# Low parts of weight tiles by ScalarE and an accumulating DMA in place of VectorE's subtraction

## The chip, the cores and the metric

The kernel runs on one core of a Trainium2 chip. The metric is device time in microseconds of one execution, as the median of three runs. The engines are named as the profile names them: PE (TensorE), with PEld for its weight loads, DVE (VectorE), ACT (ScalarE), POOL (GpSimd) and SP (SyncE, which issues most DMAs).

## The reference

A decoder trunk of two layers over 512 tokens and a width of 1024, all in float32. The first layer mixes tokens with a gated delta rule (DeltaNet), the second with sliding-window attention over one shared key/value projection; each layer ends in a gated MLP with a width-3 causal convolution. What matters here are the large products with weights:

```python
proj = hn @ w_in                       # 1024 x 6176, then conv, delta rule, gate
o @ w_out                              # 2048 x 1024
kv = rmsnorm(h, kv_norm_w) @ w_kv      # 1024 x 512
q = hn @ w_q;  o @ w_o                 # 1024 x 1024 each
u = causal_dwconv(hn @ w_up, conv_w, conv_b)          # 1024 x 5632, twice
gate, val = jnp.split(u, 2, axis=-1)
(jax.nn.silu(gate) * val) @ w_down                    # 2816 x 1024, twice
```

## The kernel before

Activations lie transposed: features on the 128 partitions, the 512 tokens along the free dimension. A float32 product is made of three products in the rounded type float32r. Every operand is split into a high part (rounded to float32r) and a low part (what the rounding left), and `mm3` adds high x high, weight high x activation low, and weight low x activation high into one PSUM bank.

Weights are streamed. `load_stage` lets SP load a block of up to 1024 x 256 weights into a buffer named `stage` (two buffers), as up to eight row blocks of 128. `cast` makes from one half of it (128 output columns) the tiles `whi` and `wlo` (three buffers each): ACT rounds to `whi`, DVE subtracts `whi` from the stage and writes `wlo`. `mm3` then runs three matmuls of 128x512 for each row block, 24 for a tile of eight. The down-projection has tiles of six and of five row blocks, the others of eight. A buffer of `whi` is free again when the last matmul of its tile that reads it (L136) is done, one of `wlo` with the last at L137.

The order of the instructions on each engine is set at build time by a scheduler that works by priorities and an estimate of each instruction's time; each engine then runs its list in order and waits for semaphores. In the DeltaNet stage the table `ORDER` and the shifts `SHIFT` set the priorities of the jobs. POOL has little to do before: it clears tiles, among them parts of `Xg` (L572) in the triangular solve, which it may do only once the matmuls at L555 have read them, and key tiles of attention (L960, L961).

Of the kernel before, what the change touches and what calls it, by code (L numbers as in the profile page):

```python
# [8 lines left out]
F32 = mybir.dt.float32  # L9
F32R = mybir.dt.float32r  # L10
BF16 = mybir.dt.bfloat16
AF = mybir.ActivationFunctionType
ALU = mybir.AluOpType
# [4 lines left out]
P = 128  # L18
# [23 lines left out]
def kernel(  # L42
# [27 lines left out]
    V, S, G, PE, SP = nc.vector, nc.scalar, nc.gpsimd, nc.tensor, nc.sync  # L70
# [6 lines left out]
    def nm(s):  # L77
        cnt[0] += 1
        return f"{s}_{cnt[0]}"
# [33 lines left out]
        return cp.tile(list(shape), dt, name=nm(s))  # L113


    def load_stage(w, r0, kt, c0):
        st = wpool.tile([P, 8, 256], F32, tag="stage", bufs=2, name=nm("stage"))
        SP.dma_start(
            st[:, :kt, :],
            w[r0 : r0 + kt * P, c0 : c0 + 256].rearrange("(k p) c -> p k c", p=P),  # L120
        )
        return st

    def cast(st, kt, half, m=P):
        hi = wpool.tile([P, 8, P], F32R, tag="whi", bufs=3, name=nm("whi"))
        lo = wpool.tile([P, 8, P], F32R, tag="wlo", bufs=3, name=nm("wlo"))
        src = st[:, :kt, half * P : half * P + m]
        S.copy(hi[:, :kt, :m], src)  # L128
        V.tensor_tensor(lo[:, :kt, :m], src, hi[:, :kt, :m].bitcast(F32), op=ALU.subtract)  # L129
        return hi, lo  # L130

# [101 lines left out]
    st = [{} for _ in range(4)]  # L233
    def project(c0, i):
        if c0 not in held_stage:
            held_stage[c0] = load_stage(win, 0, 8, c0)
        ps = bank("d")
        mm3(ps[:], cast(held_stage[c0], 8, i), KD, xh, xl)
        return ps
# [13 lines left out]
    S.dma_start(gst[:, :, 0:16], win[:, c_b : c_b + 16].rearrange("(k p) c -> p k c", p=P))  # L253
    S.dma_start(gst[:, :, 32:48], win[:, c_b + 16 : c_b + 32].rearrange("(k p) c -> p k c", p=P))
    gw = cast(gst, KD, 0, m=48)
    gps = bank("d")
    mm3(gps[:48, :], gw, KD, xh, xl, m=48)
# [518 lines left out]
    for m2 in range(KD // 2):  # L776
        sts = [load_stage(a_w_out[0], 1024 * u, 8, 256 * m2) for u in range(2)]
        for j in range(2):
            m = 2 * m2 + j
            ps = bank("d")  # L780
            for u in range(2):
                w = cast(sts[u], 8, j)
                mm3(ps[:], w, 8, yh[8 * u : 8 * u + 8], yl[8 * u : 8 * u + 8], first=u == 0, last=u == 1)
            V.tensor_tensor(hT[m], hT[m], ps[:], op=ALU.add)
# [44 lines left out]
    def ffn(l, h, last=False):  # L829
# [22 lines left out]
        for t0, t1 in ((0, 12), (12, 22)):  # L852
            gh, gl = [], []
            for t in range(t0, t1, 2):
                if l == 0 and t == 6:
                    bias_rows()
                sg = load_stage(wup, 0, 8, t * P)
                sv = load_stage(wup, 0, 8, DFF + t * P)
                gp, lp = wide("G"), wide("L")
                for j in range(2):  # L860
                    a = up(cast(sg, 8, j), t + j, "ga")
                    S.activation(a[:], a[:], AF.Silu)  # L862
                    b = up(cast(sv, 8, j), NF + t + j, "va")
                    V.tensor_tensor(b[:], a[:], b[:], op=ALU.mult)
                    split(b[:], gp[:, j, :], lp[:, j, :])
                    gh.append(gp[:, j, :])
                    gl.append(lp[:, j, :])
            ku = (t1 - t0) // 2
            for m2 in range(KD // 2):
                sts = [load_stage(wdn, (t0 + u * ku) * P, ku, 256 * m2) for u in range(2)]  # L870
                for j in range(2):
                    m = 2 * m2 + j
                    ws = [cast(sts[u], ku, j) for u in range(2)]
                    if last and t1 == NF and m == KD - 1:
                        final(h, lambda ps, ts, u: down(ps, ws, ku, gh, gl, ts, u))
                        continue
                    ps = bank("d")
                    for u in range(2):
                        down(ps[:], ws, ku, gh, gl, slice(0, T), u)
                    V.tensor_tensor(h[m], h[m], ps[:], op=ALU.add)  # L880
# [247 lines left out]
```

## Time and profile before

| | |
|---|---|
| median of 3 runs | 1462.74 us (1460.52 to 1462.97) |
| the profiled execution | 1458.21 us, of which the span 1456.4 us |
| PE busy | 1432.3 us (98%) |
| DVE busy | 953.5 us (65%) |
| ACT busy | 718.9 us (49%) |
| POOL busy | 20.1 us (1%) |
| DMA, mean over the span | 105 GB/s |
| HBM read / written | 134.65 MB / 16.80 MB |
| granted TensorE clock, mean | 0.996 |

Busy times of different engines overlap, so they don't add up to the span. A line of a group gives source line, engine, operation, output<-inputs, shape and count, then the busy time and the mean of one, then how long the engine stood idle just before these instructions and who ended that. A line of waits gives the engine and what it wanted to do, whom it waited for, the total, the number of waits and the longest. The DMA share is the mean busy share of the core's 16 DMA engines; packets whose times overlap can bring it over 100%.

### The profile page before, as it was taken

What the parts mean: (1) busy time and instruction counts of PE and PEld (TensorE: products, weight loads), DVE (VectorE), ACT (ScalarE), POOL (GpSimd) and SP (SyncE); (2) the same over time, 40 slices, a digit from 0 to 9 for tenths busy, and PEclk for the clock granted to TensorE, in tenths of its full rate; (3) what the DMA queues carried; (4) which work ended last, traced back from release to release, by engine and by line L of the source; (5) the groups of instructions that cost most, each with busy time, mean ns of one, the idle gap of its engine ahead of it and who ended that gap; (6) DMA issues with size and microseconds to landing.
All of it is one profiled execution on the core that took longest, in us unless ns stands there. A gap on an engine that the chain in (4) does not pass through costs nothing.

```text
span 1456.4 us, 19545 instructions
## 1 busy us (share of the span) xinstructions
PE 1432.3 (98%) x7519; PEld 1163.6 (80%) x7519; DVE 953.5 (65%) x1661; ACT 718.9 (49%) x1406; POOL 20.1 (1%) x47
## 2 busy tenths in 40 slices
PE   7999999999999999999999999999999999999998
PEld 5778877888877788888888888877788888888887
DVE  5896885978844436776247765777757774366754
ACT  7764564656646424443224444578744443234433
POOL 1000000000000000000010000000000000000000
PEclk9999999999999999999999999999999999999999
DMA  5334254163366523232232234221132322322222
GB/s 154 92 99 112 78 171 119 59 189 110 98 189 209 163 87 108 69 114 87 87 116 91 83 95 130 89 79 44 58 105 69 116 83 86 122 87 87 94 73 94
DMA packets 163074, 152.71 MB, mean 105 GB/s; under 512 B 24165, under 2 KB 150694, under 8 KB 162982
## 3 DMA queue, kind: packets, MB, share of 16 engines
q1 hardware_dynamic: 160722, 151.27, 33.3%
q8 instruction: 59, 0.97, 0.3%
q10 hardware_dynamic: 2259, 0.20, 0.2%
q14 instruction: 34, 0.27, 0.1%
HBM read 134.65 MB, written 16.80 MB: 104 GB/s over the span
## 4 chain that ended last, share of the span: by engine, by line
PE 95%; DMA 3%; ACT 1%; DVE 1%; issue 0%; ACTq 0%; DVEq 0%; SPq 0%
PE d L135 27%; PE d L137 27%; PE d L136 26%; PE s L585 2%; PE p L1043 1%; PE s L600 1%; PE g L1038 1%; PE s L625 1%; PE p L608 1%; PE s L562 1%; PE p L555 1%; PE s L1013 1%; PE g L450 1%; PE g L671 1%; PE g L375 1%; DMA ol<-od 0%
## 5 line engine op out<-in xcount | busy, mean ns | idle before, releaser
L135 PE MATMUL d<-xh,whi 128*128 128x512 f32 x1192 | 475.8, 400 | 0.1
L137 PE MATMUL d<-xh,wlo 128*128 128x512 f32 x1192 | 473.3, 398 | 0.0
L136 PE MATMUL d<-xl,whi 128*128 128x512 f32 x1192 | 471.6, 396 | 0.0
L128 ACT CAST whi<-stage 128x1024 fp32r<-128x1024 f32 (+2 forms) x236 | 230.5, 979 | 337.6 <-PE d L136 318.6
L129 DVE TENSOR_TENSOR wlo<-stage,whi 128x1024 fp32r<-128x1024 f32 (+2 forms) x236 | 267.3, 1133 | 120.4 <-ACT whi L128 114.3
L137 PEld LDWEIGHTS d<-xh,wlo 128*128 128x128 f32 x1192 | 224.4, 188 | 50.5 <-issue 1.4
L136 PEld LDWEIGHTS d<-xl,whi 128*128 128x128 f32 x1192 | 224.3, 188 | 48.2 <-issue 1.2
L135 PEld LDWEIGHTS d<-xh,whi 128*128 128x128 f32 x1192 | 224.7, 188 | 46.1 <-issue 0.7
L842 DVE TENSOR_TENSOR sz<-d,p6s 128x512 f32<-128x512 f32 x58 | 40.0, 689 | 62.9 <-PE d L137 61.0
L227 DVE SCALAR_TENSOR_TENSOR acc<-d,cwc,acc 128x511 f32<-128x511 f32 (+2 forms) x96 | 70.7, 740 | 9.3 <-ACT acc L224 8.8
L862 ACT ACTIVATE dt<-dt 128x512 f32<-128x512 f32 x44 | 27.8, 632 | 83.5 <-DVE dt L847 83.5
L135 PE MATMUL d<-sy,whi 128*128 128x512 f32 (+1 forms) x148 | 57.6, 390 | 0.0
L137 PE MATMUL d<-sy,wlo 128*128 128x512 f32 (+1 forms) x148 | 57.5, 389 | 0.0
L135 PE MATMUL d<-kT,whi 128*128 128x512 f32 (+1 forms) x146 | 57.5, 396 | 0.0
L136 PE MATMUL d<-sy,whi 128*128 128x512 f32 (+1 forms) x148 | 57.0, 385 | 0.0
L137 PE MATMUL d<-kT,wlo 128*128 128x512 f32 (+1 forms) x146 | 57.0, 390 | 0.0
L136 PE MATMUL d<-qT,whi 128*128 128x512 f32 (+1 forms) x146 | 56.8, 389 | 0.0
L847 DVE SCALAR_TENSOR_TENSOR va<-sz,fcw,va 128x511 f32<-128x511 f32 (+1 forms) x58 | 43.4, 748 | 2.7 <-ACT va L845 1.7
L847 DVE SCALAR_TENSOR_TENSOR dt<-sz,fcw,dt 128x511 f32<-128x511 f32 (+1 forms) x58 | 43.4, 748 | 1.2 <-ACT dt L845 0.2
L842 DVE TENSOR_TENSOR zl<-d,p6s 128x512 f32<-128x512 f32 x30 | 20.7, 689 | 33.4 <-PE d L137 33.1
L507 DVE TENSOR_TENSOR sT<-sT,p6s 64x31 f32<-64x31 f32 (+15 forms) x124 | 40.9, 330 | 2.0
L501 DVE TENSOR_TENSOR p6s<-sN,sT 64x31 f32<-64x31 f32 (+15 forms) x124 | 40.9, 330 | 1.8
(377 smaller groups left out, 2116.8 us busy)
## 6 DMA issues: line engine op xcount, KB each, us to landing
stage<-in_ffn_w_up_dram SPq DMA_DIRECT2D x44, 1024.0 KB, 5.1
stage<-in_a_w_in_dram SPq DMA_DIRECT2D x23, 1024.0 KB, 5.4
stage<-in_ffn_w_down_dram SPq DMA_DIRECT2D x16, 768.0 KB, 4.3
stage<-in_ffn_w_down_dram SPq DMA_DIRECT2D x16, 640.0 KB, 4.1
stage<-in_a_w_out_dram SPq DMA_DIRECT2D x8, 1024.0 KB, 5.0
zd<-sz SPq DMA_DIRECT2D x16, 256.0 KB, 2.1
od<-o SPq DMA_DIRECT2D x16, 256.0 KB, 2.5
stage<-in_b_w_q_dram SPq DMA_DIRECT2D x4, 1024.0 KB, 5.0
```

The source lines that it names most:

```text
L128: S.copy(hi[:, :kt, :m], src)
L129: V.tensor_tensor(lo[:, :kt, :m], src, hi[:, :kt, :m].bitcast(F32), op=ALU.subtract)
L135: PE.matmul(ps, hi[:, k, :m], xh[k], start=first and k == 0, stop=False)
L136: PE.matmul(ps, hi[:, k, :m], xl[k][:], start=False, stop=False)
L137: PE.matmul(ps, lo[:, k, :m], xh[k], start=False, stop=last and k == kt - 1)
L227: V.scalar_tensor_tensor(acc[:, d:], ps[:, : T - d], col, acc[:, d:], op0=ALU.mult, op1=ALU.add)
L501: V.tensor_tensor(tv, N[:, s, s + 1 : 32].unsqueeze(2).to_broadcast([64, n, m]), Tm[:, s : s + 1, 0:m].to_broadcast([64, n, m]), op=ALU.mult,)
L507: V.tensor_tensor(Tm[:, s + 1 : 32, 0:m], Tm[:, s + 1 : 32, 0:m], tv, op=ALU.subtract)
L585: PE.matmul(x[:, si], t[:, i, cs], S0[:, si], start=True, stop=True)
L842: V.tensor_tensor(u[:], ps[:], rs[:], op=ALU.mult)
L847: V.scalar_tensor_tensor(acc[:, d:], u[:, : T - d], tap(2 - d, t), acc[:, d:], op0=ALU.mult, op1=ALU.add)
L862: S.activation(a[:], a[:], AF.Silu)
```

## The change

`load_stage` remembers where in HBM a stage came from. `cast` no longer subtracts on DVE: ACT, after rounding to `whi`, makes a second pass that writes the negative of `whi` into `wlo`, and POOL issues a DMA that reads the same weights from HBM a second time and adds them to `wlo` in place. The first stage, which is loaded in two halves, and the small tile of gate weights keep DVE's subtraction. The weights reach the DMA in runs of 128 float32, 512 bytes, where a stage load has runs of 256.

```diff
+    origin = {}
+
     def load_stage(w, r0, kt, c0):
         st = wpool.tile([P, 8, 256], F32, tag="stage", bufs=2, name=nm("stage"))
-        SP.dma_start(
-            st[:, :kt, :],
-            w[r0 : r0 + kt * P, c0 : c0 + 256].rearrange("(k p) c -> p k c", p=P),
-        )
+        src = w[r0 : r0 + kt * P, c0 : c0 + 256].rearrange("(k p) c -> p k c", p=P)
+        SP.dma_start(st[:, :kt, :], src)
+        origin[id(st)] = (st, src)
         return st
...
         src = st[:, :kt, half * P : half * P + m]
         S.copy(hi[:, :kt, :m], src)
+        if id(st) in origin and m == P:
+            S.activation(lo[:, :kt, :m], hi[:, :kt, :m].bitcast(F32), AF.Copy, scale=-1.0)
+            G.dma_start(lo[:, :kt, :m], origin[id(st)][1][:, :, half * P : half * P + m], accum_op=ALU.add)
+            return hi, lo
         V.tensor_tensor(lo[:, :kt, :m], src, hi[:, :kt, :m].bitcast(F32), op=ALU.subtract)
```

Lines from L128 on move down by one to five: the cast of `whi` is L129 after the change, the negation L131, the DMA L132, and `mm3` L140 to L142.

ACT's list in the first layer's up-projections, before (`va`, `dt` are the convolved value and gate rows, `kT`, `sy` take rounded results):

```order
L128 CAST whi_5884<-stage_5804 128x1024
L845 ACTIVATE va_5797<-sz_5795,normc_101,fcw_371 128x512
L140 CAST kT_5654<-va_5797 128x512
L128 CAST whi_5920<-stage_5806 128x1024
L845 ACTIVATE dt_5841<-zl_5839,normc_101,fcw_371 128x512
L862 ACTIVATE dt_5841<-dt_5841 128x512
```

The same place after:

```order
L129 CAST whi_5964<-stage_5882 128x1024
L850 ACTIVATE va_5875<-sz_5873,normc_101,fcw_371 128x512
L131 ACTIVATE wlo_5965<-whi_5964 128x1024
L145 CAST kT_5728<-va_5875 128x512
L129 CAST whi_6001<-stage_5884 128x1024
L850 ACTIVATE dt_5920<-zl_5918,normc_101,fcw_371 128x512
L131 ACTIVATE wlo_6002<-whi_6001 128x1024
L867 ACTIVATE dt_5920<-dt_5920 128x512
```

The negation stands behind the next activation of the convolution, not directly behind its cast.

POOL's list at the end of the DeltaNet stage, after (before, the two clearings of `Xg` follow each other with nothing between them and the next clearing):

```order
L132 DMA wlo_4450<-in_a_w_in_dram 128x8x128
L132 DMA wlo_4679<-in_a_w_out_dram 128x8x128
L577 MEMSET Xg 32x8x32 x2
L132 DMA wlo_4708<-in_a_w_out_dram 128x8x128
L132 DMA wlo_4739<-in_a_w_out_dram 128x8x128
```

The DMAs of the low parts share POOL's queue with the clearings, which wait for PE.

## The prediction

> **What bounds the kernel now.** I read the page first (shares of the span and the chain that ended last), then the busy time by stage, then the groups of the two conversion lines, then one period of the timeline, and last the DMA queues.
>
> ```profile
> span 1456.4 us, 19545 instructions
> PE 1432.3 (98%) x7519; PEld 1163.6 (80%) x7519; DVE 953.5 (65%) x1661; ACT 718.9 (49%) x1406; POOL 20.1 (1%) x47
> PE 95%; DMA 3%; ACT 1%; DVE 1%; issue 0%; ACTq 0%; DVEq 0%; SPq 0%
> ```
>
> TensorE is busy for 98% of the span and carries 95% of the chain. Only 1456.4 - 1432.3 = 24.1 us are not its own. The stretches below are the DeltaNet stage, a stretch of up-projections, one of down-projections, and the attention heads.
>
> ```profile
> 0.00:450.00 450.00, 436.12 (x2907) 356.91 (x2908) 336.91 (x713) 273.66 (x666) 11.74 (x31) 0.99 0.42 125
> 530.00:660.00 130.00, 130.00 (x570) 105.66 (x569) 85.39 (x109) 54.93 (x69) 0.00 (x0) 1.00 0.30 95
> 660.00:740.00 80.00, 80.00 (x351) 65.65 (x350) 36.61 (x46) 22.81 (x29) 0.00 (x0) 1.00 0.31 100
> 960.00:1050.00 90.00, 90.00 (x577) 66.02 (x574) 67.40 (x219) 70.39 (x219) 0.00 (x0) 1.00 0.16 48
> ```
>
> The columns are busy PE, PEld, DVE, ACT and POOL, the granted clock, the DMA share and GB/s. In the two middle rows PE never idles at clock 1.00; 570 matmuls in 130 us are 228 ns each. The kernel is bound by the rate of its matmuls, so work taken from DVE buys almost nothing by itself. What matters is whether the new way of making a low part still arrives before its matmuls.
>
> **What is taken out and put in.** These groups are the rounding on ACT and the subtraction on DVE, by shape:
>
> ```profile
> L128 ACT CAST whi<-stage 128x1024 fp32r<-128x1024 f32 x172 | 180.4, 1052 | 193.0 <-PE d L136 178.4 <-DMA stage<-in_a_w_in_dram 4.2 <-issue 4.0
> L128 ACT CAST whi<-stage 128x768 fp32r<-128x768 f32 x32 | 26.8, 836 | 84.2 <-PE d L136 84.2
> L128 ACT CAST whi<-stage 128x640 fp32r<-128x640 f32 x32 | 23.3, 729 | 60.4 <-PE d L136 56.0 <-PE d L137 3.0 <-DMA stage<-in_ffn_w_down_dram 1.4
> L129 DVE TENSOR_TENSOR wlo<-stage,whi 128x1024 fp32r<-128x1024 f32 x172 | 210.3, 1224 | 64.0 <-ACT whi L128 58.2 <-PE d L135 1.6 <-PE d L137 0.3
> L129 DVE TENSOR_TENSOR wlo<-stage,whi 128x768 fp32r<-128x768 f32 x32 | 30.7, 958 | 38.1 <-ACT whi L128 38.0
> L129 DVE TENSOR_TENSOR wlo<-stage,whi 128x640 fp32r<-128x640 f32 x32 | 26.3, 822 | 18.2 <-ACT whi L128 18.0
> ```
>
> 234 tiles change: 170 of eight row blocks, 32 of six, 32 of five (the first two tiles and the small gate tile keep the subtraction). DVE loses 170 x 1.224 + 32 x 0.958 + 32 x 0.822 = 265 us. ACT gains a pass of the same shapes; taken at the price of the cast it is 170 x 1.052 + 32 x 0.836 + 32 x 0.729 = 229 us, so ACT goes to 948 us, 65% of the span. Its densest stretch, the attention heads, holds 8 of these tiles: (70.4 + 8 x 1.05)/90 = 88%. As PE is fully busy there, I cost the ACT pass itself at 0; its cover is the two tiles that are ready ahead, and if that were gone it would be the 8.4 us of that stretch. What DVE's relief can return is at most PE's waits for DVE:
>
> ```profile
> PE g L314 <- DVE sz L282: 2.5, 1, 2.5
> PE g L774 <- DVE va L672: 2.5, 1, 2.5
> PE s L585 <- DVE S L611: 0.8, 1, 0.8
> PE d L908 <- DVE xh L922: 0.2, 1, 0.2
> PE s L213 <- DVE xl L145: 0.2, 1, 0.2
> PE g L927 <- DVE ol L923: 0.2, 1, 0.2
> ```
>
> That is 6.4 us in all, between 0 and -6.4; I take 0, since the long ones wait for a chain of which DVE is one link. SP's loads wait less long for a free stage buffer:
>
> ```profile
> SPq L118 <- DVE wlo L129: 852.0, 99, 29.6
> ```
>
> They will now wait for ACT's cast, about 1.2 us earlier. PE waits for no stage, so this is worth 0.
>
> **The new path of a low part.** One period of an up-projection, then two casts each of the six- and five-block down-projections:
>
> ```profile
> 604.05 1.05 ACT L128 CAST whi<-stage 128x1024 fp32r<-128x1024 f32 x1 [1.00 <-PE d L136]
> 605.01 0.82 ACT L845 ACTIVATE va<-sz,normc,fcw 128x512 f32<-128x512 f32 x1
> 609.54 1.05 ACT L128 CAST whi<-stage 128x1024 fp32r<-128x1024 f32 x1 [0.35 <-PE d L136]
> ...
> 605.14 1.23 DVE L129 TENSOR_TENSOR wlo<-stage,whi 128x1024 fp32r<-128x1024 f32 x1 [0.17 <-ACT whi L128]
> ...
> 693.90 0.84 ACT L128 CAST whi<-stage 128x768 fp32r<-128x768 f32 x1 [3.33 <-PE d L136]
> 697.98 0.84 ACT L128 CAST whi<-stage 128x768 fp32r<-128x768 f32 x1 [3.23 <-PE d L136]
> ...
> 898.54 0.73 ACT L128 CAST whi<-stage 128x640 fp32r<-128x640 f32 x1 [2.71 <-PE d L136]
> 901.97 0.73 ACT L128 CAST whi<-stage 128x640 fp32r<-128x640 f32 x1 [1.29 <-PE d L136]
> ```
>
> Each cast starts when PE lets go of its buffer, so PE's time per tile is 609.54 - 604.05 = 5.49 us, 4.08 and 3.43. With three buffers a tile has two such periods until its matmuls: 11.0, 8.2 and 6.9 us. DVE finished the low part at 606.37, 2.3 us after the start. Now comes the cast, in the up stage the activation that the new order puts between, and the negation: 1.05 + 0.82 + 1.05 = 2.92 us (1.67 and 1.46 in the down stages, where I count no activation between); then POOL issues, and the transfer must land. Left for issue and transfer: 8.1, 6.5 and 5.4 us. What lands later stops PE, since its matmuls are in a fixed order, and with PE the release of the next buffer, ACT's next cast and POOL's next issue.
>
> The trace has no DMA issued by POOL and none that adds. The nearest rows are plain loads, first queue 1 in 600 to 650 us (pieces of 1 KB) and in 9 to 11 us (pieces of 512 B, the size of the new ones), then issue to landing of three loads:
>
> ```profile
> q1 hardware_dynamic: 5228, 5.27, 33.2%
> ...
> q1 hardware_dynamic: 1150, 0.58, 121.3%
> ...
> stage<-in_ffn_w_up_dram SPq DMA_DIRECT2D x44, 1024.0 KB, 5.1
> stage<-in_ffn_w_down_dram SPq DMA_DIRECT2D x16, 768.0 KB, 4.3
> stage<-in_ffn_w_down_dram SPq DMA_DIRECT2D x16, 640.0 KB, 4.1
> ```
>
> A 1 KB piece occupies an engine for 0.332 x 50 x 16 / 5228 = 50.8 ns, a 512 B piece for 1.213 x 2 x 16 / 1150 = 33.8 ns. A load of 1024 pieces over 16 engines is 3.25 us of work, so of its 5.1 us 1.85 are fixed (1.86 and 2.07 from the others; I take 1.9). An added tile has 1024 pieces. If adding costs what a copy costs, the work is 1024 x 33.8 ns / 16 = 2.16 us (lower end); if reading the weights, reading the tile and writing it are each charged as a copy, 6.49 us (upper end). No row is near enough to choose; I take the middle, two copies: 4.33 us for eight blocks, 3.24 for six, 2.70 for five.
>
> POOL's part is bounded by these rows:
>
> ```profile
> L118 SPq DMA_DIRECT2D stage<-in_ffn_w_up_dram x44: 367/368/377, 527.5 to 1353.6; - x44
> L336 POOL MEMSET Xg<- 128x2048 f32 x1 | 1.8, 1801 | 0.0
> L572 POOL MEMSET Xg<- 32x256 f32 x8 | 2.4, 304 | 399.9 <-PE p L555 399.9
> ```
>
> An issue on SP takes 0.37 us, POOL's longest writing instruction 1.80; I take their middle, 1.1 us for every size, and keep in mind that the true end may lie far above both. The third row shows the queue that the new DMAs share: POOL stood 399.9 us before the eight clearings of Xg. A DMA queued behind one starts late, but in the new order at least 28 rows of PE work stand between the matmuls that free Xg and that tile's first use, so I cost this at 0 (upper end: the 46 tiles of the DeltaNet stage at the same 0.47 us as below, 22 us). At 450/46 = 9.8 us per tile, that stage is not short of transfer time.
>
> **The sum.** Two limits hold for a tile's period. First the engines: half a stage load per tile (1.63, 1.22, 1.02 us) plus the added transfer gives 5.96, 4.46 and 3.72 us, against PE's 5.49, 4.08 and 3.43. Then a third of a buffer's round (use, ACT, POOL, fixed part, transfer and half a load met on the way): (5.49 + 2.92 + 1.1 + 1.9 + 4.33 + 1.63)/3 = 5.79, (4.08 + 1.67 + 1.1 + 1.9 + 3.24 + 1.22)/3 = 4.40 and 3.87. The larger of each pair exceeds PE by 0.47, 0.38 and 0.44 us. In dense stages stand 88 up, 16 out, 4 key/value and 8 output tiles: 116 x 0.47 = 54.5; 32 x 0.38 = 12.2; 32 x 0.44 = 14.1; together 81 us. The 8 query tiles lie among attention work, 0. The profiled execution took 1458.2 us; the median of the runs is 4.5 above. 1458.2 + 81 + 4.5 = 1544 us.
>
> **Rivals.** (a) The transfer is hidden and nothing changes. With one copy's price the engines need 2.16 + 1.63 = 3.79 us per tile, and issue to landing 1.1 + 1.9 + 2.16 + 1.63 = 6.8 us against 8.1 in the up stage (5.8 against 6.5 and 5.4 against 5.4 in the others): 1463 us. The low DMA share of 0.30 speaks for it; that the new pieces are the small ones and that the five-block stage has nothing left speaks against. The Trainium skill, "DMA: Bandwidth & Descriptors", section "Anatomy of one DMA — SWDGE (gpsimd) path", fits a DMA issued by GpSimd as 2.0 us plus its bytes at 436 GB/s, 3.2 us for 512 KB; by that rule this rival would win. No run here shows such a DMA, and the plain 640 KB load took 4.1 us where the rule gives 3.5.
>
> (b) Faster: rival (a), and PE loses its waits for DVE too. It decides only where no low part lands later than 8.1, 6.5 and 5.4 us. It gives 1463 - 6.4 = 1456 us.
>
> (c) Much slower: POOL needs longer to issue 1024 pieces than PE needs for the tile, or adding costs three copies. Each microsecond beyond 5.49 per 1024 pieces costs 116 + 32 x 0.75 + 32 x 0.625 = 160 us, since every dense tile pays in proportion. With three copies it is 6.49 + 1.63 - 5.49 = 2.63 us, 421 us, 1884 us; POOL at 8 us would give 402 us, 1865. For it: 1024 pieces is half the count of words per partition that POOL's MEMSET writes in 1.80 us, and a piece is more than a word. Against it: no row shows the price. The same page of the Trainium skill, section "SWDGE vs HWDGE vs iDMA", says that for a GpSimd-issued DMA a core computes the descriptors in software; it gives no time for one, and no trace of before shows it.
>
> **Chances.** Forecast, 1480 to 1620 us: 0.42. Rival (c), 1620 upward: 0.36, with 0.08 above 1890. Rival (a): 0.17, of which 0.05 as a small loss up to 1480. Rival (b): 0.05. A change under 0.2% cannot be told from none here. So faster 0.05, same 0.12, slower 0.83. The range from 1460 to 1890 leaves out (b) and the far end of (c).
>
> **What would show it.** PE's waits should name DMA into wlo at L137, in the up and down stretches and hardly before 450 us, and 570 matmuls should take some 141 us instead of 130. The DMA share in the up stretch should come near 0.9; about 0.6 would be rival (a). ACT should stand near 948 us and DVE near 689. If POOL's queue is occupied for more than 5.5 us per DMA while the share stays low, (c) by POOL is right; if the new pieces cost over 68 ns each, (c) by the adding. I would be wrong altogether if PE still is at 228 ns per matmul in the up stretch.

## The result and the profile after

The changed kernel takes 1592.87 us (median of 4 runs, 1589.88 to 1601.18), beside 1461.63 us for the kernel before, run on the same chip. Over all runs it is 1.0916 times as long, with a 95% interval of 1.0863 to 1.0969. The forecast was 1544 us, a loss of 81 us where 131 were measured. The direction and the order of size are right. The place is not, as the profile shows.

The head of the page of the changed kernel, the first line of its chain, and the queue of the DMAs that POOL issues:

```profile
span 1589.8 us, 20082 instructions
PE 1487.4 (94%) x7519; PEld 1194.2 (75%) x7519; DVE 720.5 (45%) x1427; ACT 927.1 (58%) x1640; POOL 378.3 (24%) x281
...
q0 software_dynamic: 222880, 112.21, 57.0%
...
issue 36%; PE 35%; POOL 13%; DMA 12%; ACT 2%; DVE 2%; POOLq 0%; ACTq 0%; SPq 0%; DVEq 0%
```

The span grew by 133.4 us. PE stands idle for 1589.8 - 1487.4 = 102.4 us instead of 24.1, 78 more. It is also busy for 55 us more with the same 7519 matmuls, so matmuls became slower. PE's share of the chain fell from 95% to 35%, and POOL, which was not in it, has 13%.

The stretches by time, first of before, then of after, in the columns that the prediction explains. The whole front of the kernel, up to the first up-projection (the DeltaNet stage and its output projection, together "the mixer" from here on), was not shown yet for before:

```profile
0.00:550.80 550.80, 533.28 (x3345) 434.61 (x3346) 381.95 (x770) 317.56 (x743) 11.74 (x31) 0.99 0.43 128
```

```profile
0.00:650.10 650.10, 575.36 (x3342) 461.93 (x3343) 316.48 (x705) 379.77 (x808) 111.36 (x95) 0.91 0.78 160
650.10:760.00 109.90, 109.87 (x481) 89.41 (x482) 55.86 (x80) 66.33 (x80) 31.05 (x20) 1.00 1.01 186
760.00:852.00 92.00, 90.59 (x391) 72.72 (x390) 20.29 (x29) 42.89 (x52) 30.88 (x24) 1.00 1.04 186
1080.00:1160.00 80.00, 80.00 (x512) 59.14 (x511) 61.02 (x210) 71.72 (x219) 9.31 (x6) 1.00 0.49 93
```

The mixer ends at 650.1 us instead of 550.8 with as many matmuls (3342 and 3345 in the records): 99 of the 133 us are lost there. The rest is 20 us in the first MLP with the key/value projection, 7 us in the attention output and 7 us in the second MLP. The second row is an up stretch. PE is busy for all of it, at 109.87/481 = 228 ns per matmul, as before. There the transfers are hidden, although the DMA share is 1.01. The heads (last row) keep clock 1.00 and lose nothing.

The new instructions on ACT and POOL, by group, and the time from issue to landing of their DMAs:

```profile
L131 ACT ACTIVATE wlo<-whi 128x1024 fp32r<-128x1024 f32 (+2 forms) x234 | 229.6, 983 | 2.8
L132 POOL DMA_DIRECT2D wlo<-in_ffn_w_up_dram x88 | 136.6, 1553 | 344.8 <-ACT wlo L131 344.6
L132 POOL DMA_DIRECT2D wlo<-in_a_w_in_dram x46 | 71.6, 1575 | 358.6 <-ACT wlo L131 258.3
```

```profile
wlo<-in_ffn_w_up_dram POOLq DMA_DIRECT2D x88, 512.0 KB, 6.5
...
wlo<-in_a_w_in_dram POOLq DMA_DIRECT2D x46, 512.0 KB, 7.3
...
wlo<-in_ffn_w_down_dram POOLq DMA_DIRECT2D x32, 384.0 KB, 5.7
...
wlo<-in_ffn_w_down_dram POOLq DMA_DIRECT2D x32, 320.0 KB, 5.7
```

POOL holds each DMA for 1.55 us, and the low part lands 6.5 us after POOL begins in the up stages, 7.3 in the DeltaNet stage. POOL's idle time is mostly waiting for ACT's negation (258.3 of 358.6 us for `a_w_in`), so POOL is not the bound. The waits of PE now name the low parts, and DeltaNet's `a_w_in` first:

```profile
PE d L142 <- DMA wlo<-in_a_w_in_dram: 29.2, 8, 7.8
PE d L142 <- DMA wlo<-in_ffn_w_down_dram: 15.6, 13, 4.1
PE d L142 <- DMA wlo<-in_a_w_out_dram: 13.2, 3, 6.9
```

One of the eight waits for `a_w_in`, from the timeline of ACT, then POOL, then PE:

```profile
285.33 1.05 ACT L129 CAST whi<-stage 128x1024 fp32r<-128x1024 f32 x1 [1.38 <-PE d L141]
...
291.57 1.28 ACT L673 ACTIVATE ol<-ol,fc 128x128 f32<-128x128 f32 x4 [1.71 <-DMA ol<-od]
292.76 0.67 ACT L229 ACTIVATE acc<-d,cwc 128x512 f32<-128x512 f32 x1
293.33 0.58 ACT L661 ACTIVATE sz<-d 128x512 f32<-128x512 f32 x1
293.81 1.05 ACT L131 ACTIVATE wlo<-whi 128x1024 fp32r<-128x1024 f32 x1
...
295.21 1.55 POOL L132 DMA_DIRECT2D wlo<-in_a_w_in_dram  x1 [10.92 <-ACT wlo L131]
...
296.58 0.40 PE L141 MATMUL d<-xl,whi 128*128 128x512 f32 x1
301.89 0.80 PE L142 MATMUL d<-xh,wlo 128*128 128x512 f32 x1 [4.91 <-DMA wlo<-in_a_w_in_dram]
302.48 0.63 PE L140 MATMUL d<-xh,whi 128*128 128x512 f32 x1
```

The cast to `whi` ran at 285.33, but the negation stands in ACT's list behind work of the delta rule, part of which waits for a DMA of its own. It starts 8.5 us after its cast. POOL issues at 295.21, the low part lands at 301.9, and PE has stood for 4.91 us.

Paired tile by tile in the order of their lists, the waits for `a_w_in` and `a_w_out` in the mixer, eleven with 42.4 us, each end as one low part lands. They have two origins. In five of them, 21.1 us in all, the negation starts 8.1 to 14.8 us after its cast, as in the timeline above. In the other six, 21.3 us, it starts 1.1 to 3.6 us after it, and the transfer and the short distance to the first use remain: two of the three `a_w_out` tiles land 8.8 and 11.1 us after POOL's issue. The landing time of 7.3 us is a median. POOL's issues at 297.69 and 300.14 us, right behind that of 295.21, take 11.2 and 11.7 us to land. The spread over the DeltaNet stage, then over an up stretch of the kernel that changes the up tiles alone (below):

```profile
DMA to landing us min/median/max: 6.1/7.3/13.0
```

```profile
DMA to landing us min/median/max: 6.1/6.5/7.7
```

After the stall the matmuls are slow: 0.63 us long instead of 0.39. The clock of the same microseconds, one row each:

```profile
301.00:302.00 1.00, 0.11 (x1) 0.12 (x1) 0.90 (x4) 0.00 (x0) 0.69 (x1) 0.50 1.10 355
304.00:305.00 1.00, 1.00 (x3) 0.76 (x3) 0.92 (x3) 0.00 (x0) 0.00 (x0) 0.50 1.21 262
306.00:307.00 1.00, 1.00 (x6) 0.83 (x5) 0.91 (x3) 0.00 (x0) 0.00 (x0) 1.00 1.42 198
```

The granted clock is 0.50 until about 306 us, some 4 us after PE began again, with three or four matmuls started per microsecond instead of six at 1.00 (the share of "busy" hides this). So a stall costs a second time. This is where PE's extra busy time comes from. The Trainium skill, "TensorE: Matmul & The Clock Gate", section "What's actually happening", says that TensorE falls to half rate after an idle window of some 3.4 us and is released after about as long at work. This trace agrees with it only in part. The release of this stall, some 4 us, fits. But PE's last matmul before it ended at 296.98, and the clock is at 0.50 from 299.1, 2.1 us later; at 193.3 it falls after a wait of 1.88 us. And the release can take far longer, as after the wait of 2.66 us that ended at 136.21:

```profile
135.30:159.10 23.80, 22.89 (x160) 18.11 (x161) 4.81 (x9) 3.35 (x8) 2.37 (x3) 0.50 0.63 113
```

PE is busy for 22.89 of these 23.8 us and stays at 0.50 throughout; the same happens from 486.9 to 510.7, after a wait of 2.1 us for ACT (L673). Why these two last so long, no run shows.

### The profile page after: what moved, and what is told of

It reads as the page before. It is cut to its first block, busy times and chain, and to the rows that moved or that the text cites. A ratio compares the mean times of both kernels' runs of the same rounds, so it can differ in the third digit from the quotient of the medians.

```text
span 1589.8 us, 20082 instructions
## 1 busy us (share of the span) xinstructions
PE 1487.4 (94%) x7519; PEld 1194.2 (75%) x7519; DVE 720.5 (45%) x1427; ACT 927.1 (58%) x1640; POOL 378.3 (24%) x281
## 3 DMA queue, kind: packets, MB, share of 16 engines
q0 software_dynamic: 222880, 112.21, 57.0%
## 4 chain that ended last, share of the span: by engine, by line
issue 36%; PE 35%; POOL 13%; DMA 12%; ACT 2%; DVE 2%; POOLq 0%; ACTq 0%; SPq 0%; DVEq 0%
POOL wlo L132 13%; PE d L142 8%; PE d L140 8%; PE d L141 8%; DMA wlo<-in_a_w_in_dram 3%; DMA wlo<-in_ffn_w_down_dram 3%; DMA wlo<-in_a_w_out_dram 1%; DMA ol<-od 1%; PE p L1048 1%; PE g L1043 1%; PE s L590 1%; DMA stage<-in_a_w_in_dram 1%; PE s L605 1%; PE s L567 1%; ACT wlo L131 1%
## 5 line engine op out<-in xcount | busy, mean ns | idle before, releaser
L142 PE MATMUL d<-xh,wlo 128*128 128x512 f32 x1192 | 481.2, 405 | 31.6 <-DMA wlo<-in_a_w_in_dram 29.2
L140 PE MATMUL d<-xh,whi 128*128 128x512 f32 x1192 | 481.9, 405 | 7.8 <-DVE acc L232 3.8
L141 PE MATMUL d<-xl,whi 128*128 128x512 f32 x1192 | 479.3, 403 | 0.0
L129 ACT CAST whi<-stage 128x1024 fp32r<-128x1024 f32 (+2 forms) x236 | 230.1, 978 | 365.4 <-PE d L141 345.8
L142 PEld LDWEIGHTS d<-xh,wlo 128*128 128x128 f32 x1192 | 228.7, 192 | 85.3 <-DMA wlo<-in_a_w_in_dram 32.4
L140 PEld LDWEIGHTS d<-xh,whi 128*128 128x128 f32 x1192 | 228.8, 192 | 57.3 <-ACT whi L129 7.8
L131 ACT ACTIVATE wlo<-whi 128x1024 fp32r<-128x1024 f32 (+2 forms) x234 | 229.6, 983 | 2.8
L132 POOL DMA_DIRECT2D wlo<-in_ffn_w_up_dram x88 | 136.6, 1553 | 344.8 <-ACT wlo L131 344.6
L132 POOL DMA_DIRECT2D wlo<-in_a_w_in_dram x46 | 71.6, 1575 | 358.6 <-ACT wlo L131 258.3
L132 POOL DMA_DIRECT2D wlo<-in_ffn_w_down_dram x64 | 94.0, 1469 | 174.4 <-ACT wlo L131 174.4
L232 DVE SCALAR_TENSOR_TENSOR acc<-d,cwc,acc 128x509 f32<-128x509 f32 (+2 forms) x96 | 71.0, 742 | 40.6 <-ACT acc L229 39.5
L142 PE MATMUL d<-kT,wlo 128*128 128x512 f32 (+1 forms) x146 | 59.6, 408 | 8.8 <-DMA wlo<-in_a_w_out_dram 6.9
L142 PE MATMUL d<-sy,wlo 128*128 128x512 f32 (+1 forms) x148 | 58.3, 394 | 6.3 <-DMA wlo<-in_a_w_out_dram 6.3
L140 PE MATMUL d<-kT,whi 128*128 128x512 f32 (+1 forms) x146 | 58.4, 404 | 0.0
L140 PE MATMUL d<-sy,whi 128*128 128x512 f32 (+1 forms) x148 | 57.9, 392 | 0.0
L885 DVE TENSOR_TENSOR pz<-pz,d 128x512 f32<-128x512 f32 x15 | 10.3, 687 | 101.0 <-PE d L142 101.0
```

The costliest lines, as they stand in the source:

```text
L131: S.activation(lo[:, :kt, :m], hi[:, :kt, :m].bitcast(F32), AF.Copy, scale=-1.0)
L132: G.dma_start(lo[:, :kt, :m], origin[id(st)][1][:, :, half * P : half * P + m], accum_op=ALU.add)
L140: PE.matmul(ps, hi[:, k, :m], xh[k], start=first and k == 0, stop=False)
L141: PE.matmul(ps, hi[:, k, :m], xl[k][:], start=False, stop=False)
L142: PE.matmul(ps, lo[:, k, :m], xh[k], start=False, stop=last and k == kt - 1)
L232: V.scalar_tensor_tensor(acc[:, d:], ps[:, : T - d], col, acc[:, d:], op0=ALU.mult, op1=ALU.add)
```

## Experiments

Theory D says that the low part lands too late where the chain from cast to use is long, O that the order of the instruction lists, which changed with the build, costs the time. Later runs weigh further rivals: ACT's pass, the added traffic, the adding itself. Times are medians and ratios are to the kernel before, with 95% intervals. Where a stage is named, its increment is read from the one profiled run against before's. That run lies within 4 us of its kernel's median, except for all but `a_w_in` (10 us below), copying in 512 B (8 below) and the halves (8 above); differences of stages by less than this are not told apart.

**The negation alone.** The DMA is left out, so the low parts lack the weights.

```diff
-            G.dma_start(lo[:, :kt, :m], origin[id(st)][1][:, :, half * P : half * P + m], accum_op=ALU.add)
```

> Leaves out the accumulating DMA: ACT still writes the negative of the rounded part into wlo, and nothing is added, so the low parts are wrong numbers of the right shape. Theory D (the low parts come late because of POOL's issue and the transfer): within 1% of the kernel before, 1450 to 1476 us, and the stretch from the start to the first output-projection matmul back to about 435 us from 530. Rival A (ACT's second pass in its in-order list delays everything else): 1540 us or more, that stretch still above 500 us. Rival O (the scheduler's other order of the DeltaNet stage): somewhere above 1480 us, since this order also differs from the one before.

Measured 1471.77 us, 1.0085 [1.0057, 1.0112]. The mixer loses 12.5 us, all else nothing. ACT's pass and the lists built with it cost about a tenth of the loss.

**DVE writes the negative.**

```diff
-            S.activation(lo[:, :kt, :m], hi[:, :kt, :m].bitcast(F32), AF.Copy, scale=-1.0)
+            V.tensor_scalar(lo[:, :kt, :m], hi[:, :kt, :m].bitcast(F32), -1.0, None, op0=ALU.mult)
```

> The negative is written by DVE instead of ACT; POOL's accumulating DMA stays as in the change. Theory D: 1575 to 1610 us, as the change, and PE's waits still name the DMA into wlo. Rival A: 1500 us or less, since ACT is back at about 700 us of busy time. Rival O: open, as the order differs again.

Measured 1577.26 us, 1.0823 [1.0775, 1.0872]. With ACT relieved (719.5 us busy) the mixer still loses 75.9 us of the 99.3: that ACT is the engine of the negation is not the main cause. On DVE the negation stands in an ordered list as well.

**By place.** Three kernels make only some low parts in the new way: the DeltaNet stage's `a_w_in` alone, the up-projections alone, the down-projections alone. A fourth makes all but `a_w_in` so.

```diff
-        origin[id(st)] = (st, src)
...                                                          # one of these four:
+        if w is win:                                        # DeltaNet alone
+        if w is not win:                                    # all but DeltaNet
+        if w.tensor.name.startswith('in_ffn_w_up'):         # up alone
+        if w.tensor.name.startswith('in_ffn_w_down'):       # down alone
+            origin[id(st)] = (st, src)
```

> The mirror of the last: only the tiles of a_w_in get their low part by ACT and the accumulating DMA. Independent stages: 1545 to 1565 us, all of the loss before the first output-projection matmul. If the DeltaNet stage loses because of traffic of other stages' low parts (it overlaps with little), under 1500 us.

> The tiles of a_w_in (46 of 234, the DeltaNet stage) keep DVE's subtraction, all others as in the change. By the landmarks of the two traces the DeltaNet stage lost 95 of the 133 us: if the stages are independent, 1490 to 1505 us, with the rest of the loss (about 38 us) in the output projection and the down-projections. If the loss of the DeltaNet stage was only pushed there by the start of the next stage, 1530 us or more.

> Only the 88 up-projection tiles use the accumulating DMA; the lists of the other stages are those of before. By the trace of the change (PE at 220 matmuls per 50 us there) it is hidden: 1455 to 1468 us. By the step of the prediction (0.47 us per tile) it would be 1500 us.

> Only the 64 down-projection tiles use the accumulating DMA; the lists of the other stages are those of before. By the prediction's step (12.2 + 14.1 us) and by the landmarks of the change (20 + 7 us in the two MLPs): 1480 to 1495 us, with the waits in the five-block half above all. If the loss there came from the up-projection's traffic next to it, under 1470 us.

| | median, us | ratio | where it is lost |
|---|---|---|---|
| `a_w_in` alone | 1539.42 | 1.0547 [1.0517, 1.0577] | mixer +80.0, then nothing |
| all but `a_w_in` | 1531.77 | 1.0511 [1.0485, 1.0536] | mixer +32.3, first MLP and key/value +16.7, attention output +6.9, second MLP +8.1 |
| up alone | 1458.82 | 1.0012 [0.9985, 1.0038] | nothing |
| down alone | 1486.35 | 1.0178 [1.0128, 1.0229] | first MLP +20.4, second +10.8 |

"Up alone" keeps the lists of before elsewhere; its up stretch and its landing time, then the landings and PE's weight-load waits of "down alone":

```profile
530.00:660.00 130.00, 129.96 (x569) 105.69 (x569) 61.59 (x87) 76.17 (x92) 34.30 (x22) 1.00 0.97 178
```

```profile
wlo<-in_ffn_w_up_dram POOLq DMA_DIRECT2D x88, 512.0 KB, 6.6
```

```profile
wlo<-in_ffn_w_down_dram POOLq DMA_DIRECT2D x32, 384.0 KB, 6.1
...
wlo<-in_ffn_w_down_dram POOLq DMA_DIRECT2D x32, 320.0 KB, 5.8
```

```profile
PEld d L143 <- DMA wlo<-in_ffn_w_down_dram: 27.3, 24, 3.7
```

A transfer of the same size is hidden in the up stage, where it lands in 6.6 us, and costs 80 us in the DeltaNet stage. In the up stage 88 of the 234 tiles cost nothing: 569 matmuls in 130 us, as before. The down tiles come out near their forecast. "`a_w_in` alone" came out 6 us below the range expected of it. "All but `a_w_in`" was a miss, forecast too low: with it the mixer loses 32 us, most of it at the 16 tiles of the DeltaNet output projection, which follow the last delta-rule work. PE waits for them three times, 20.0 us in all; the rest is mostly slower matmuls. The two kernels don't add up (80.0 + 32.3 against 99.3), since each has lists of its own: in the change, what the output tiles add is 19.3 us by difference.

**Copying and adding, small and large pieces.** The instruction lists of these kernels are those of the change on every engine. `copy` drops the adding (the weights overwrite the negative). `big` adds, but from the top rows of the tile's matrix, in pieces of 4 KB (3 and 2.5 KB for the down tiles), not from the tile's own weights (all but the key/value tiles). `copy_big` does both.

```diff
-            G.dma_start(lo[:, :kt, :m], origin[id(st)][1][:, :, half * P : half * P + m], accum_op=ALU.add)
+            G.dma_start(lo[:, :kt, :m], origin[id(st)][1][:, :, half * P : half * P + m])                   # copy
...                                                                                                     # where a row of the matrix is long enough:
+                G.dma_start(lo[:, :kt, :].rearrange("p k c -> p (k c)"), wb[0:P, 0 : kt * P], accum_op=ALU.add)    # big
+                G.dma_start(lo[:, :kt, :].rearrange("p k c -> p (k c)"), wb[0:P, 0 : kt * P])                      # copy_big
```

> The same lists of instructions as the change on every engine, but POOL's DMA copies instead of adding (the low parts are then the whole weights). Theory D (the low part lands too late for the place its matmuls have): the landing shrinks from 6.5 to 7.3 us to some 4.5, the down-projections lose nothing more, the DeltaNet stage loses 50 to 70 us instead of 93: 1510 to 1540 us. Theory O (the scheduler's other order of the DeltaNet stage costs the time, whatever the landing): the DeltaNet stage stays at 85 us or more lost, 1550 us or more.

> Same lists again and still adding as many bytes, but in runs of 4 KB from the top rows of the weight matrix instead of runs of 512 bytes, so other weights are added (the four key/value tiles keep their own). If the piece size makes the transfer long, the work falls from 4.2 to some 2.6 us per tile and the time lies between the copy and the change, 1520 to 1560 us; if the adding of the bytes sets it, within 1% of the change.

> The same lists as the change; POOL's DMA copies, and in runs of 4 KB from the top rows of the matrix (the low parts are then other weights). The least transfer that these lists allow. Theory D: the landing in the DeltaNet stage falls below the copy's 5.5 us, to about 4.5, and its loss from 49 to some 25 us: 1495 to 1515 us. Theory O: what is lost does not follow the landing any more, 1520 us or more.

The landing of the `a_w_in` tiles in `copy` and POOL's group there, then the landing in `big` and in `copy_big`:

```profile
wlo<-in_a_w_in_dram POOLq DMA_DIRECT2D x46, 512.0 KB, 5.5
```

```profile
L132 POOL DMA_DIRECT2D wlo<-in_a_w_in_dram x46 | 40.4, 877 | 353.1 <-ACT wlo L131 249.2 <-PE s L605 30.6 <-PE s L547 22.4
```

```profile
wlo<-in_a_w_in_dram POOLq DMA_DIRECT2D x46, 512.0 KB, 6.6
```

```profile
wlo<-in_a_w_in_dram POOLq DMA_DIRECT2D x46, 512.0 KB, 4.8
```

| | landing, up / `a_w_in`, us | mixer, us | median, us | ratio |
|---|---|---|---|---|
| adding, 512 B (the change) | 6.5 / 7.3 | +99.3 | 1592.87 | 1.0916 [1.0863, 1.0969] |
| adding, 4 KB | 5.8 / 6.6 | +89.5 | 1579.71 | 1.0812 [1.0749, 1.0876] |
| copying, 512 B | 4.9 / 5.5 | +47.3 | 1525.64 | 1.0454 [1.0382, 1.0526] |
| copying, 4 KB | 4.3 / 4.8 | +52.3 | 1514.43 | 1.0391 [1.0368, 1.0414] |

Adding costs 1.8 us of landing at either piece size in the DeltaNet stage, and half of the loss of the whole kernel, 67 us at 512 B and 65 at 4 KB by the medians (in the mixer of the profiled runs 52 and 37). Larger pieces shorten the landing by 0.7 us and gain 11 to 13 us. `big` came out within 1% of the change, the sign named for the adding and against the pieces. Since the lists are the same, O cannot explain the 67 us between the change and `copy`. Whether D alone is enough stays open. Between the two copying kernels the landing fell by 0.7 us and the mixer of the profiled runs did not gain, but the profiled run of `copy` is the fastest of its four, and the intervals of the two ratios overlap. The time of copying in 4 KB runs lies inside the span that was named for D, at its upper end; the loss of the stage does not, with 52 us against the 25 named.

**The negation moved forward, and tiles cut in two.** In the first, the program lets ACT write the negative of the rounded stage directly and POOL issue before ACT writes `whi`. In the second, `wlo` is besides two tiles of four row blocks with a negation and a DMA each, so that the first half may land earlier.

```diff
+            S.activation(lo[:, :kt, :m], src, AF.Copy, scale=-1.0)     # then the DMA, then the cast
+            G.dma_start(lo[:, :kt, :m], origin[id(st)][1][:, :, half * P : half * P + m], accum_op=ALU.add)
+            S.copy(hi[:, :kt, :m], src)
```

> ACT writes the negative first, straight from the stage (rounding the negated weight), POOL's DMA follows, and the high part is cast after it; otherwise the change. The transfer can start a cast earlier, and in the DeltaNet stage by the rows that stand between cast and negation in ACT's list of the change (4.0 on the mean, now 0.4). Theory D: the DeltaNet stage's loss falls from 93 to 50 to 70 us, the five-block tiles' loss by more than half: 1525 to 1555 us. If the place on ACT's list is of no account, within 1% of the change.

> As the last, and each low tile is made as two tiles of four row blocks (six buffers of half the size), each with its own negation and DMA: a half lands sooner, and the second half is needed 2.7 us after the first. Theory D: less lost than with the negative first alone, 1490 to 1530 us. If POOL's second issue (1.55 us each, if it does not shrink with the size) or ACT's fixed cost per pass outweighs it, no better than the last or worse.

Measured 1582.13 us, 1.0847 [1.0816, 1.0878], and 1547.01 us, 1.0609 [1.0592, 1.0627]. Both were misses for D; the first is within 1% of the change, the sign that the place on ACT's list is of no account. But this kernel does not test it fully. The rows between the cast and the negation fall from 4.0 to 0.4 on average in the DeltaNet stage, and the mixer still loses 80.6 us. Yet the scheduler may still set a negation behind its cast, and the traces, paired in the order of the lists, show it at 18 of the 46 tiles, by up to 13.0 us. Three of the eight waits that remain, 13.5 of 29.3 us, are at such tiles, whose negation comes 8.8 to 13.0 us after the cast; PE waits at the same three in the change. One of them, the cast on ACT, its negation (two in one row), and PE:

```profile
277.24 1.05 ACT L132 CAST whi<-stage 128x1024 fp32r<-128x1024 f32 x1 [0.25 <-PE d L142]
...
286.07 2.00 ACT L130 ACTIVATE wlo<-stage 128x1024 fp32r<-128x1024 f32 x2
...
296.78 0.79 PE L143 MATMUL d<-xh,wlo 128*128 128x512 f32 x1 [7.90 <-DMA wlo<-in_a_w_in_dram]
```

Besides, the DMAs issued in that kernel need longer to land:

```profile
wlo<-in_a_w_in_dram POOLq DMA_DIRECT2D x46, 512.0 KB, 8.2
```

So the place on ACT's list, which the timeline above suggests as the cause, is a part of it, and the 19 us gained in the mixer do not measure how large a part. Halving the tiles helps more (mixer +59.5 us), as D says: the wait is for the first row blocks of a tile, and 256 KB arrive sooner (6.5 us) than the 512 KB of the kernel with the negation first (8.2). The order of the lists differs from the change's in both, and how much of the gain is order was not separated.

**The traffic without the wait.** The DMA carries the negative out to scratch, and no matmul waits for it.

```diff
-            G.dma_start(lo[:, :kt, :m], origin[id(st)][1][:, :, half * P : half * P + m], accum_op=ALU.add)
+            away = dp.tile([P, 8, P], F32, name=nm("away"))
+            G.dma_start(away[:, :kt, :m], lo[:, :kt, :m].bitcast(F32))
```

> POOL's DMA has 1024 pieces of 512 bytes per tile as in the change, and waits for the negation as there, but it carries the finished negative out to a scratch area in HBM; the matmuls read the negative and do not wait for the DMA (the low part lacks the weights). The instructions of PE, ACT, DVE and SP stand as in the run with the negation alone, 1472 us. What is tested is what remained of the loss in the DeltaNet stage when the landing was cut to 4.8 us (copying in 4 KB runs: still 489 us to the stage's end against 435). Theory L, the low part comes too late for its matmuls (and the order of the lists built around it): without the wait the stage ends by 440 to 455 us and the whole takes 1470 to 1490. Rival C, contention: the added traffic holds up the stage's own transfers (the triangular solve's reads and writes of scratch, 2 to 3 us before, 4 to 6 with the DMAs): then the stage ends after 475 us and the whole takes 1505 to 1540. In between, 1490 to 1505, both have a part.

```profile
0.00:571.60 571.60, 539.13 (x3342) 435.81 (x3342) 314.79 (x705) 375.75 (x806) 45.97 (x95) 0.98 0.57 182
```

Measured 1481.41 us, 1.0164 [1.0139, 1.0189]. The mixer ends at 571.6 us, 20.8 after before's and 8.3 after that with the negation alone. The DMA share of the row, 0.57, is that of the copying kernel with 4 KB runs (0.58). One thing was not as the expectation says: the scratch tile is contiguous, and the queue shows 29600 packets in place of 222880, so this is the traffic of the 4 KB kernels, not of 512-byte pieces, and it goes out to HBM, not in. Against `copy_big` it says that contention is not most of what remained there: the same volume without the wait costs 8 us, with the wait (and the other lists) 40. What the traffic of adding DMAs costs without a wait, no run shows.

## Why the prediction was right, and where it was wrong

The profiled loss of the mixer can be put together from four runs: the negation and its lists 12.5 us (negation alone); traffic that nobody waits for 571.6 - 563.3 = 8.3; waiting for a copying DMA, with the change's lists, 598.1 - 571.6 = 26.5; adding instead of copying 650.1 - 598.1 = 52.0. The sum is 99.3 us. In the third part, lateness and order stay mixed. The border between the last two is loose by some 8 us, since the profiled run of copying is that much faster than its median. The last part holds all that adding brings, the later landing and the heavier traffic.

By the prediction's steps:

- *The kernel is bound by matmuls, DVE's relief is worth 0.* Right. DVE fell to 720.5 us, and where the transfer is hidden (up alone) the time is 1.0012 of before. The forecast of 689 took the groups' sum off a busy time in which instructions overlap (before, DVE's instructions sum to 1024.8 us in 953.5 of busy time); ACT's 948 against 927.1 is off for the same reason, since the negation itself took 229.6 us of the forecast 229.
- *ACT's pass costs 0, its thin place being the attention heads.* The heads lost nothing. The pass, with the lists built for it, costs 12.5 us in the mixer, which the step did not name.
- *Prices of the transfer.* A piece was taken at 67.6 ns. In an up stretch of the trace after, queue 0 shows 19245 pieces and a share of 74.3% over 105 us: 0.743 x 105 x 16 / 19245 = 64.9 ns. POOL's issue was taken at 1.1 us and took 1.55.
- *Up stage: each of 88 tiles exceeds PE's period by 0.47 us.* This step failed: it gave 41 of the 81 us forecast, and with the up tiles alone 2 us were measured, within the noise. Both limits were too strict. The rate limit added up the times of packets, 4.33 + 1.63 = 5.96 us per tile; but packets overlap, and at a share of 1.01 PE still ran without a gap. The round added fixed part, transfer and half a stage load to POOL's 1.1, 8.96 us; they overlap, and the trace shows 6.5 us in all, less than the 8.1 us that the prediction itself had left.
- *Down stages: 12.2 + 14.1 = 26.3 us.* Measured 29.5 us in the profiled run with them alone. Here the landing of 5.8 us for five blocks exceeds the 5.4 that were left; the six-block tiles, 6.1 against 6.5, had more room.
- *16 output and 8 attention output tiles, 0.47 us each.* The latter lost 6.9 us in place of 3.8. The former were mis-sized by a factor of 2.5 to 4: 7.5 forecast, 19.3 in the change by difference, 32.3 with all but `a_w_in`. The four key/value tiles (1.9 forecast) show no loss of their own: their stretch lost 20 us in the change and with the down tiles alone.
- *DeltaNet stage: 0, at most 22 us.* This step failed the most: 80 us alone. It compared transfer time with the stage's average of 9.8 us per tile and took the cover of two periods from the dense stages. The timelines show why that cover is not there: at five of the eight waits for `a_w_in` the negation queues behind other work on ACT, part of which waits for the delta rule's transfers, and tiles come in bunches (POOL issues three DMAs between 295 and 302 us after a pause of 10.9), whose transfers take up to 13.0 us. The remark on the queue looked at POOL's waits for `Xg`; at all eleven waits POOL issued at most half a microsecond after the negation's end, and the queue that mattered was ACT's.
- *Nothing on the clock.* The forecast priced a stall at its own length. In the mixer PE idles 57.2 us more and is busy 42.1 us more, the latter at a mean clock of 0.91 instead of 0.99.

So the forecast 81 us came in the main from the wrong place: the up stage, its largest term, gave nothing, and the stage that was set to 0 gave three fifths of the loss (80 of 133 us). That the time lies inside 1480 to 1620 us is in good part luck: one wrong term stood in for another.

Rival (a), the hidden transfer, holds for the up stage, and for the attention heads. The Trainium skill's fit for a GpSimd-issued DMA ("DMA: Bandwidth & Descriptors", section "Anatomy of one DMA — SWDGE (gpsimd) path") gives 3.2 us for 512 KB; the runs show 4.3 us when it copies in 4 KB runs and 6.5 when it adds in 512-byte pieces, next to the kernel's own loads, so the measurement decides against it here, above all for adding. Rival (c) needed pieces over 68 ns or an issue over 5.49 us; neither is there. None of the versions beats the kernel before; the best of them, the up stage alone, equals it, since an idle DVE buys nothing under a busy PE.

What stays open is how the 26.5 us of waiting for a copying DMA divide between lateness and the order of the lists: no run had the change's lists with a low part that comes at once. Open too is how much the late negations cost, since no run put every negation right behind its cast or ahead of it.

## What to carry to other kernels

When an operand's way to its matmul is made longer, look for the tile whose producer stands behind other work on an in-order engine, and measure the cover there; a stage's average time per tile says nothing of tiles that come in bunches. Where a DMA share nears 1.0, test the rate by what the consumer does, not by adding up packet times. A stall of TensorE costs more than its own length: in the mixer 57 us more idle time went with 42 us of slower matmuls, and with `copy` 32 with 15, so here its price is about one and a half to one and three quarters times its length.

## What was not expected of the hardware

- After a stall of 4.91 us the granted clock was 0.50 for some 4 us of work, but after stalls of 2.66 and 2.1 us for 23.8 us of work. Over the mixer, the mean clock fell from 0.99 to 0.91 without any change of the matmuls.
- An adding DMA of 1024 pieces of 512 bytes holds POOL for 1.55 us. The same pieces copied take 0.88 us, 4 KB pieces added 0.86 and 4 KB pieces copied 0.53. Small pieces or adding alone bring a third of a microsecond, both together a whole one.
- Adding lengthened the landing of a 512 KB tile by 1.5 to 1.8 us, whatever the pieces; 0.6 to 0.7 us went to the smaller pieces.
- A mean DMA share of 1.01 to 1.04 over 90 to 110 us stood beside matmuls that lost nothing or 1.4 us, so the share, summed from packet times, did not tell here what the engines could still take.
